# Later merge pieces, an earlier query norm, and an expert choice cut in pieces, in a two-block transformer kernel

## The chip, the cores and the metric

The kernel runs on one core of one Trainium2 chip. The time is the device time of one execution, in microseconds (us). The core has five engines with queues of their own: TensorE (PE, matmuls and transposes; its weight loads are listed as PEld), VectorE (DVE), ScalarE (ACT), GpSimd (POOL in the profile) and SyncE (SP, which only issues DMAs). Each works through its own queue in order and waits on the others through semaphores.

## What is computed

Two blocks over 1024 tokens of width 1024, in float32. The first has a mixer with two branches and a layer of 32 experts; the second has another mixer and a layer of 64 experts with a shared one. Cut to what matters here:

```python
# first block
xa = causal_conv(x_rnn, conv_w, conv_b)
ya = rg_lru(xa, ...) * gelu(g_rnn)
q = rms_norm(((rms_norm(q_c) @ w_uq)).reshape(B, S, 16, 96), q_norm_g)   # 16 heads
k = rms_norm(concat([k_nope, k_pe]), k_norm_g)
q, k = rope on the last 32 of 96
yb = chunk_causal_attention(q, k, v)
merged = gates[0] * ya + gates[1] * yb
h = h + merged @ w_out
h = h + hier_moe(rms_norm(h), ...)            # 32 experts in 4 groups, top 2
# second block
mix = concat([hgrn2(q, k, v, f) normed and gated, multiscale_pool(u) @ w_pool])
h = layer_norm(h * ALPHA + mix @ w_out)
scores = sigmoid(h @ w_router); sel = scores + bias
# the 4 best of 8 groups, then the 8 best experts in them, weights normed
h = layer_norm(h * ALPHA + moe_ffn(h))        # 64 experts, top 8, and a shared expert
```

## The kernel before

The stages follow one another, each with its own pools of tiles; a tile in a new pool lies where older ones lay and waits for their last readers. Each engine runs its instructions in the order of the program text, with semaphores between the engines. Products in which precision matters are made of three float32r matmuls (`mm3`): each operand is split in a high part (a rounding copy, mostly on ACT, L247) and a low part (the difference, mostly on DVE, L253).

**Queries and keys.** Eight chunks of weights, keys and queries in turn, are multiplied with the latents; each chunk gives 4 heads for 1024 tokens. The norm of a chunk's half (`post_q`) is a generator of a few steps: mean square, root, scaling and rope, and the store to `q_d` on SP. The steps are taken one at a time between later tiles. The function that holds all this is itself a generator: it yields once, attention sets up and does its first head, and then it goes on. In the kernel before the yield comes ahead of the last steps, and the last half's rope is on DVE; the others are on GpSimd.

**Attention.** It loads k, q and v of a pair of heads (`load`), reads the norm weights of q and k into `gk`, splits transposed pieces (`t_piece`), and computes for head n + 1 the maxima of the scores (`m_piece`, tile tm, reduces into nm on DVE) beside the scores of head n. A head has eight tile rows kt; for each, `s_mm` makes scores in PSUM (st, three buffers) and ACT takes the exps (L950). `row_piece` (L929) closes the maxima of a head, once in each head's period. After an odd head, the pair before is merged with the gates and the recurrent branch in six parts: 0 and 1 scale by 1/sum, 2 and 3 apply the gates (DVE, L994 and L996), 4 copies the result to mgh (ACT, two of 128x512, L999), 5 writes the remainder mgl (DVE, L1002). The table MERGE says for each part from which head on and at which kt; `rec` fetches the next head's 1/sum.

**First expert layer.** The route runs on DVE while the first expert's weights, loaded ahead, are split in six pieces (four of gate and up, two of down). START and ORDER say how many pieces stand ahead of each step of the route and in which order the rest goes (s a piece, o one-hot tables, w the second columns of the slot table, x transposes); LOD0 names the pieces whose low part is made on DVE, the others are on GpSimd.

**Second mixer and its projection.** `mixer2` has pools hc (v and others), hw (weights) and more; they lie where the staging tiles s0 to s2 of w_out come to lie again. `mixer_out2` loads w_out through these tiles in eight pieces (s, L2388, split to woh and wol), and goes over ten steps t: two half tiles of the product and the sum with the residual (L2461), `trans(t - 2)` behind the first and `router(t - 2)` behind the second, then `norm(t)`, whose root is on ACT (rsa_t, L291). `route2` chooses experts for four token tiles at a time; for tiles 0 to 3 it runs whole behind router(3).

Of the kernel before, what the change touches and what calls it, by code (L numbers as in the profile page):

```python
# [231 lines left out]
class Body:  # L232
# [429 lines left out]
    def qkv(self):  # L662
# [5 lines left out]
        with ExitStack() as cx:  # L668
# [111 lines left out]
            for i in range(8):  # L780
# [27 lines left out]
                else:  # L808
                    qn = ep.tile([128, 8, 4, 96], F32, name="qn", tag="kq", bufs=3)
                    dst = self.q_d[c].rearrange("(t p) c -> p t c", p=128)  # L810
                    for t in range(8):
# [11 lines left out]
                            step()  # L823
                        if t == 3:
                            posts.append(post_q(qn, sq, 0, dst, nc.gpsimd))
                    posts.append(post_q(qn, sq, 4, dst, nc.vector if i == 7 else nc.gpsimd))
            pc.close()
            yield
            while posts:
                step()  # L830

    MERGE = (2, 0), (3, 0), (3, 0), (3, 1), (3, 1), (3, 2)

    def attention(self, rb, rk, ml):

# [3 lines left out]
        with ExitStack() as cx:  # L839
# [37 lines left out]
            room(1)  # L877
            load(0)
            load(1)
            gk = k0.tile([96, 3], F32, name="gk")  # L880
            for i, nme in enumerate(("q_norm_g", "k_norm_g")):
                a = IN[nme]
                nc.scalar.dma_start(gk[:, i:i + 1], bass.AP(tensor=a.tensor, offset=a.offset, ap=[[1, 96], [1, 1]]))
            sc = 96 ** -0.5
            nc.vector.memset(gk[64:96, 0:2], 1.0)
            nc.vector.tensor_mul(gk[:, 2:3], gk[:, 0:1], gk[:, 1:2])
# [180 lines left out]
            def beside(h, kt):  # L1067

                n = h + 1
                fill = []  # L1070
                if kt == 0 and h % 2:
                    load(h // 2 + 2)
                if n < 16:
                    if kt < 2:
                        fill += [(t_piece, n, "kq"[kt], half) for half in range(2)]
                    fill += [(m_piece, n, i, a) for i, a in
                             {3: [(7, 0), (7, 512), (6, 0)], 4: [(6, 512), (5, 0), (5, 512)],
                              5: [(4, 0), (4, 512), (3, 0)], 6: [(2, 0), (1, 0), (0, 0)]}.get(kt, ())]
                    if kt == 5:
                        fill.append((v_piece, n))  # L1080
                    if kt == 7:
                        fill += [(lambda: None,), (row_piece, n)]
                if kt == (3 if h == 15 else 4) and h > 0:
                    fill.append((rec, h - 1))
                if h == 15 and kt == 6:
                    fill.append((merge, 7, 0, 0, 2, nc.vector))
                for part, (late, at) in enumerate(self.MERGE):
                    if h >= late and (h - late) % 2 == 0 and kt == at:
                        fill.append((merge, (h - late) // 2, part, 0, 2, nc.vector if part else nc.gpsimd))
                return fill  # L1090

            self.wo, self.W = {}, {}
# [161 lines left out]


    def moe_consts(self):
        nc, c = self.nc, self.const
        self.before = c.tile([128, 128], BF, name="before")
        nc.vector.tensor_scalar(self.before, self.jp, 0.0, None, op0=OP.is_gt)
# [692 lines left out]
    CAP1 = 96  # L1952
    RAW1, RAW2 = 13, 11
    DBUFS = 1, 1
    START, ORDER = (1, 1, 2, 0), "oswsSSx"
    YACT = 5
    LOD = (0, 2, 5), (0, 3, 5)
    LOD0 = (5,), (1, 3)

    def shared_place(self, j):  # L1960
        return self.sh.tile([128, 2048], F32, name=f"s{(j + 1) % 3}")
# [86 lines left out]
    def mixer2(self, u2):  # L2048

        nc, tc, IN = self.nc, self.tc, self.IN  # L2050
        win = IN["w_in_2"][0]
        with ExitStack() as cx:
            c1 = cx.enter_context(tc.tile_pool(reuse_waits="tile", name="hc", bufs=1))
            wp = cx.enter_context(tc.tile_pool(reuse_waits="tile", name="hw", bufs=2))
            sp = cx.enter_context(tc.tile_pool(reuse_waits="tile", name="hs", bufs=10))
            ep = cx.enter_context(tc.tile_pool(reuse_waits="tile", name="he", bufs=1))
            up = u2.enter_context(tc.tile_pool(reuse_waits="tile", name="u2", bufs=1, side="right"))
# [273 lines left out]
            self.mgh = mix.tile([128, 8, S], F32R, name="mxh")  # L2331
            self.mgl = mix.tile([128, 8, S], F32R, name="mxl")
            with tc.tile_pool(reuse_waits="tile", name="hq", bufs=2, space=PSUM) as pp, tc.tile_pool(reuse_waits="tile", name="hqt", bufs=4, space=PSUM) as pt:
                wpl = wp.tile([128, 4, 128], F32, name="w")
                nc.sync.dma_start(wpl, IN["w_pool_2"][0].rearrange("g c d -> c g d"))
                wplh = wp.tile([128, 4, 128], F32R, name="wh")
                wpll = wp.tile([128, 4, 128], F32R, name="wl")
                self.split(wpl, wplh, wpll)
                hg = c1.tile([128, 4], F32, name="hg")
                nc.vector.tensor_scalar(hg, self.v("hg_norm_g_2", 0, 4), 0.5, None, op0=OP.mult)  # L2340
# [25 lines left out]
    def mixer_out2(self, mo):  # L2366
# [5 lines left out]
        with ExitStack() as cx:  # L2372
# [58 lines left out]
            def router(t):  # L2431
                xT, xf = X.pop(("T", t)), X.pop(("f", t))
                pl = pt.tile([128, 512], F32, name="tp")
                for k in range(8):
                    nc.tensor.matmul(pl[:, 0:64], xT[:, k], rw[:, k], start=k == 0, stop=k == 7)
                nc.scalar.activation(lg[t // 4][:, t % 4], pl[:, 0:64], AF.Copy)
                ah = ep.tile([128, D], F32, name="ah", bufs=1)
                nc.scalar.activation(self.plain(ah), self.turned(xf), AF.Copy, scale=self.ALPHA)
                (nc.gpsimd if t > 4 else nc.sync).dma_start(self.acc_d[t * 128:t * 128 + 128], ah)
                if t == 3:  # L2440
                    for _ in self.route2(rtp, lg[0], bias, 0, 4):
                        pass
            self.route_late = lambda rp: self.route2(rp, lg[1], bias, 4, 8)
            self.pre2 = {}

# [2 lines left out]
            for t in range(10):  # L2448
# [4 lines left out]
                for half in range(2):  # L2453
                    if t < 8:
# [4 lines left out]
                                     [(self.mgh[:, k, ts_], self.mgl[:, k, ts_], h[:, k], lo[:, k]) for k in range(8)])  # L2459
                        hs = X[t][:, half * 512:half * 512 + 512]  # L2460
                        nc.vector.scalar_tensor_tensor(hs, hs, self.ALPHA, ps, op0=OP.mult, op1=OP.add)  # L2461
                    if t > 1:
                        (router if half else trans)(t - 2)
                if t < 8:
                    norm(t)
                    loadx(t + 2)


    def route2(self, rp, lg, bias, t0, t1):
# [286 lines left out]
```

## Time and profile before

| | us |
|---|---|
| three runs | 3194.46, 3202.43, 3207.52; median 3202.43 |
| the profiled execution | 3195.43 |
| its span in the trace | 3193.6 |

The stages, by the trace: recurrent branch to 475, latents to 570, queries and keys to 722, attention to about 1075, output projection and first route to 1229, 32 experts to 1586, second mixer to 1970, its projection to 2121, 64 experts to 3160, and the last norms.

In the rows, PEclk is the clock that TensorE was granted as a share of full speed; a matmul at half clock takes up to twice as long. "idle before <- X" names what ended the engine's idle time just before the instruction. Buffer numbers are left out of names.

### The profile page before, as it was taken

Reading aid. Unit: us, or ns where it says so; the run is one execution under the profiler, and the core shown is the slowest. Engines: PE = TensorE matmul, PEld = TensorE weight load, DVE = VectorE, ACT = ScalarE, POOL = GpSimd, SP = SyncE. Lnnn points to the kernel's source line nnn. Section 1 sums busy time; section 2 is a strip of 40 time slices with the busy share of each in tenths; the row PEclk is TensorE's granted clock in tenths of the full one; section 3 lists DMA queues with packets and bytes.
Section 4 is the critical chain, followed back from the end, with each engine's and each line's share of the span. In section 5 each row is a group of like instructions: output and inputs, shape, how many; then the busy total and the mean of one; then the engine's idle time right before and its main releaser. Section 6 shows DMA issues by size and latency. Waiting matters only on the chain. (4 is left out here: it accounts for less than half of the span.)

```text
span 3193.6 us, 41876 instructions
## 1 busy us (share of the span) xinstructions
PE 2953.0 (92%) x15865; PEld 2183.8 (68%) x15865; DVE 1814.7 (57%) x2909; ACT 1249.6 (39%) x1929; POOL 642.9 (20%) x495
## 2 busy tenths in 40 slices
PE   5999999998999996999889998978999999999995
PEld 4778778896666893655479787955666666666663
DVE  5545651666666656566446565445655555555556
ACT  3332332444445323444343324332344444444343
POOL 0000000121000103233212232112233232333320
PEclk9999999998999997999989999979999999999997
DMA  3212120244332267999720102337899999999994
GB/s 115 66 53 86 66 73 23 97 163 110 93 93 90 92 219 275 300 330 351 239 104 28 40 18 90 132 137 242 267 282 322 303 327 313 316 316 323 314 307 144
DMA packets 225885, 579.71 MB, mean 182 GB/s; under 512 B 22421, under 2 KB 104005, under 8 KB 225653
## 3 DMA queue, kind: packets, MB, share of 16 engines
q1 hardware_dynamic: 187952, 444.37, 39.6%
q0 software_dynamic: 37296, 132.55, 16.6%
q8 instruction: 127, 2.08, 0.3%
q14 instruction: 78, 0.64, 0.1%
q10 hardware_dynamic: 432, 0.06, 0.0%
HBM read 470.22 MB, written 106.64 MB: 181 GB/s over the span
## 5 line engine op out<-in xcount | busy, mean ns | idle before, releaser
L271 PE MATMUL mm<-uh,wh 128*128 128x512 f32 x640 | 252.6, 395 | 10.8 <-ACT t L505 8.8
L273 PE MATMUL mm<-uh,wl 128*128 128x512 f32 x640 | 251.8, 393 | 0.0
L272 PE MATMUL mm<-ul,wh 128*128 128x512 f32 x640 | 251.7, 393 | 0.0
L1475 PE MATMUL gups<-raw,x 128*128 128x512 f32 (+1 forms) x536 | 236.4, 592 | 0.0
L1622 ACT ACTIVATE th<-gups 128x128 f32<-128x128 f32 (+2 forms) x136 | 49.0, 361 | 418.9 <-PE gups L1475 251.0
L1691 POOL DMA_INDIRECT acc_d<-y,si x68 | 118.3, 1740 | 438.9 <-DMA acc_d<-y,si 145.9
L1623 DVE SCALAR_TENSOR_TENSOR hh<-th,gups 128x128 f32<-128x128 f32 (+2 forms) x136 | 53.1, 390 | 241.9 <-ACT th L1622 235.7
L253 DVE TENSOR_TENSOR gl<-raw,gh 128x1024 fp32r<-128x1024 f32 x142 | 168.1, 1221 | 28.4 <-ACT gh L247 28.3
L1688 DVE TENSOR_SCALAR y<-yps,wsl 128x512 f32<-128x512 f32 (+1 forms) x95 | 71.2, 750 | 196.7 <-ACT y L1686 193.8
L271 PE MATMUL gups<-gh,xh 128*128 128x512 f32 (+1 forms) x440 | 179.8, 409 | 0.9 <-ACT xh L1589 0.9
L1686 ACT ACTIVATE y<-yps,wsl 128x512 f32<-128x512 f32 (+1 forms) x100 | 68.7, 687 | 276.9 <-PE yps L1475 146.9
L273 PE MATMUL gups<-gh,xl 128*128 128x512 f32 (+1 forms) x440 | 176.4, 401 | 0.0
L272 PE MATMUL gups<-gl,xh 128*128 128x512 f32 (+1 forms) x440 | 176.1, 400 | 0.0
L1475 PEld LDWEIGHTS gups<-raw,x 128*128 128x128 f32 (+1 forms) x536 | 95.3, 183 | 116.4 <-issue 116.4
L1579 PEld LDWEIGHTS tp<-ident,xg 128*128 128x128 f32 (+2 forms) x1088 | 114.2, 144 | 74.6 <-issue 38.5
L958 PE MATMUL o<-raw,v 128*128 128x512 f32 (+3 forms) x384 | 163.4, 514 | 0.0
L271 PEld LDWEIGHTS mm<-uh,wh 128*128 128x128 f32 x640 | 121.7, 190 | 38.1 <-ACT t L505 10.6
L247 ACT ACTIVATE gh<-raw 128x1024 fp32r<-128x1024 f32 x142 | 142.9, 1054 | 10.5 <-PE gups L273 7.7
L1579 PE MATMUL tp<-ident,xg 128*128 128x128 f32 (+2 forms) x1088 | 128.5, 262 | 15.5 <-DMA xg<-xf_d,gi 7.1
L273 PEld LDWEIGHTS mm<-uh,wl 128*128 128x128 f32 x640 | 121.6, 190 | 25.7
L272 PEld LDWEIGHTS mm<-ul,wh 128*128 128x128 f32 x640 | 121.7, 190 | 25.3
L950 ACT ACTIVATE raw<-st 128x512 f32<-128x512 f32 (+1 forms) x192 | 92.8, 490 | 117.8 <-PE st L949 116.7
(685 smaller groups left out, 7669.0 us busy)
## 6 DMA issues: line engine op xcount, KB each, us to landing
raw<-in_w_down_dram SPq DMA_DIRECT2D x69, 1024.0 KB
raw<-in_w_gate_dram SPq DMA_DIRECT2D x136, 512.0 KB
raw<-in_w_up_dram SPq DMA_DIRECT2D x136, 512.0 KB
w<-in_w_in_dram SPq DMA_DIRECT2D x20, 1024.0 KB
s<-in_w_down_dram SPq DMA_DIRECT2D x17, 1024.0 KB
s<-in_w_gate_dram SPq DMA_DIRECT2D x34, 512.0 KB
s<-in_w_up_dram SPq DMA_DIRECT2D x34, 512.0 KB
b<-in_w_gate_dram SPq DMA_DIRECT2D x22, 512.0 KB
```

Source lines behind the costliest of these rows:

```text
L247: nc.scalar.activation(hi, src, AF.Copy)
L253: e.tensor_tensor(lo, src, hi.bitcast(F32), op=OP.subtract)
L271: nc.tensor.matmul(out, lh, rh, start=start and i == 0, stop=False, **kw)
L272: nc.tensor.matmul(out, lh, rl, start=False, stop=False, **kw)
L273: nc.tensor.matmul(out, ll, rh, start=False, stop=stop and i == n - 1, **kw)
L950: nc.scalar.activation(raw[:, a - kt * 128:b - kt * 128], st, AF.Exp)
L958: nc.tensor.matmul(O[h][a // 512][:, a % 512:a % 512 + b - a], v, p[:, a - kt * 128:b - kt * 128], start=kt == 0, stop=kt == (7 if a >= 51 ...
L1475: nc.tensor.matmul(out, x, w, start=start and i == 0, stop=stop and i == len(pairs) - 1, **kw)
L1579: nc.tensor.transpose(ps[:, k // 4, (k % 4) * R:(k % 4) * R + R], xg[:R, k * 128:k * 128 + 128], self.ident[:R, :R])
L1686: nc.scalar.activation(y[:R, 0:512], ps[0][:R], AF.Copy, scale=w)
L1688: nc.vector.tensor_scalar(y[:R, 512:1024], ps[1][:R], w, None, op0=OP.mult)
L1691: nc.gpsimd.indirect_dma_start(out=acc_d, out_offset=bass.IndirectOffsetOnAxis(ap=si, axis=0), in_=y[:R], in_offset=None, compute_op=OP.add)
```

## The change

Five things change.

1. MERGE: part 4 moves from kt 1 to kt 3 and part 5 from kt 2 to kt 4; in one kt the merge's parts now stand ahead of `rec`.
2. The last steps of the norms of q stand ahead of the yield, the last half's rope is on GpSimd like the others, and gk's loads move to the setup.
3. START, ORDER and LOD0: the first expert's pieces 0 and 1 stand at the route's start with low parts on GpSimd, pieces 2 to 5 have theirs on DVE. The pieces of expert 1 (S) are gone from ORDER; expert 1 is split whole in both kernels.
4. In mixer2 the pool hw is opened ahead of hc, and the pooling weights go through a slot of another pool instead of hw.
5. In mixer_out2 the expert choice of tiles 0 to 3 is taken in pieces: three steps after norm(5), three after norm(6), the rest in step 7; trans(6) stands ahead of norm(7).

```diff
--- before.py
+++ after.py
@@ -823,13 +823,13 @@
                             step()
                         if t == 3:
                             posts.append(post_q(qn, sq, 0, dst, nc.gpsimd))
-                    posts.append(post_q(qn, sq, 4, dst, nc.vector if i == 7 else nc.gpsimd))
+                    posts.append(post_q(qn, sq, 4, dst, nc.gpsimd))
             pc.close()
-            yield
             while posts:
                 step()
-
-    MERGE = (2, 0), (3, 0), (3, 0), (3, 1), (3, 1), (3, 2)
+            yield
+
+    MERGE = (2, 0), (3, 0), (3, 0), (3, 1), (3, 3), (3, 4)
 
     def attention(self, rb, rk, ml):
 
@@ -877,10 +877,7 @@
             room(1)
             load(0)
             load(1)
-            gk = k0.tile([96, 3], F32, name="gk")
-            for i, nme in enumerate(("q_norm_g", "k_norm_g")):
-                a = IN[nme]
-                nc.scalar.dma_start(gk[:, i:i + 1], bass.AP(tensor=a.tensor, offset=a.offset, ap=[[1, 96], [1, 1]]))
+            gk = self.gk
             sc = 96 ** -0.5
             nc.vector.memset(gk[64:96, 0:2], 1.0)
             nc.vector.tensor_mul(gk[:, 2:3], gk[:, 0:1], gk[:, 1:2])
@@ -1080,13 +1077,13 @@
                         fill.append((v_piece, n))
                     if kt == 7:
                         fill += [(lambda: None,), (row_piece, n)]
+                for part, (late, at) in enumerate(self.MERGE):
+                    if h >= late and (h - late) % 2 == 0 and kt == at:
+                        fill.append((merge, (h - late) // 2, part, 0, 2, nc.vector if part else nc.gpsimd))
                 if kt == (3 if h == 15 else 4) and h > 0:
                     fill.append((rec, h - 1))
                 if h == 15 and kt == 6:
                     fill.append((merge, 7, 0, 0, 2, nc.vector))
-                for part, (late, at) in enumerate(self.MERGE):
-                    if h >= late and (h - late) % 2 == 0 and kt == at:
-                        fill.append((merge, (h - late) // 2, part, 0, 2, nc.vector if part else nc.gpsimd))
                 return fill
 
             self.wo, self.W = {}, {}
@@ -1254,6 +1251,10 @@
 
 
     def moe_consts(self):
+        self.gk = self.const.tile([96, 3], F32, name="gk")
+        for i, nme in enumerate(("q_norm_g", "k_norm_g")):
+            a = self.IN[nme]
+            self.nc.scalar.dma_start(self.gk[:, i:i + 1], bass.AP(tensor=a.tensor, offset=a.offset, ap=[[1, 96], [1, 1]]))
         nc, c = self.nc, self.const
         self.before = c.tile([128, 128], BF, name="before")
         nc.vector.tensor_scalar(self.before, self.jp, 0.0, None, op0=OP.is_gt)
@@ -1952,10 +1953,10 @@
     CAP1 = 96
     RAW1, RAW2 = 13, 11
     DBUFS = 1, 1
-    START, ORDER = (1, 1, 2, 0), "oswsSSx"
+    START, ORDER = (2, 0, 0, 0), "osswxss"
     YACT = 5
     LOD = (0, 2, 5), (0, 3, 5)
-    LOD0 = (5,), (1, 3)
+    LOD0 = (2, 3, 4, 5), (1, 3)
 
     def shared_place(self, j):
         return self.sh.tile([128, 2048], F32, name=f"s{(j + 1) % 3}")
@@ -2050,8 +2051,9 @@
         nc, tc, IN = self.nc, self.tc, self.IN
         win = IN["w_in_2"][0]
         with ExitStack() as cx:
+
+            wp = cx.enter_context(tc.tile_pool(reuse_waits="tile", name="hw", bufs=2))
             c1 = cx.enter_context(tc.tile_pool(reuse_waits="tile", name="hc", bufs=1))
-            wp = cx.enter_context(tc.tile_pool(reuse_waits="tile", name="hw", bufs=2))
             sp = cx.enter_context(tc.tile_pool(reuse_waits="tile", name="hs", bufs=10))
             ep = cx.enter_context(tc.tile_pool(reuse_waits="tile", name="he", bufs=1))
             up = u2.enter_context(tc.tile_pool(reuse_waits="tile", name="u2", bufs=1, side="right"))
@@ -2331,10 +2333,9 @@
             self.mgh = mix.tile([128, 8, S], F32R, name="mxh")
             self.mgl = mix.tile([128, 8, S], F32R, name="mxl")
             with tc.tile_pool(reuse_waits="tile", name="hq", bufs=2, space=PSUM) as pp, tc.tile_pool(reuse_waits="tile", name="hqt", bufs=4, space=PSUM) as pt:
-                wpl = wp.tile([128, 4, 128], F32, name="w")
+                wpl = slot()[:, :512].rearrange("p (g d) -> p g d", g=4)
                 nc.sync.dma_start(wpl, IN["w_pool_2"][0].rearrange("g c d -> c g d"))
-                wplh = wp.tile([128, 4, 128], F32R, name="wh")
-                wpll = wp.tile([128, 4, 128], F32R, name="wl")
+                wplh, wpll = [z[:, a] for z in [slot(F32R).rearrange("p (a g d) -> p a g d", a=2, g=4)] for a in range(2)]
                 self.split(wpl, wplh, wpll)
                 hg = c1.tile([128, 4], F32, name="hg")
                 nc.vector.tensor_scalar(hg, self.v("hg_norm_g_2", 0, 4), 0.5, None, op0=OP.mult)
@@ -2437,9 +2438,12 @@
                 ah = ep.tile([128, D], F32, name="ah", bufs=1)
                 nc.scalar.activation(self.plain(ah), self.turned(xf), AF.Copy, scale=self.ALPHA)
                 (nc.gpsimd if t > 4 else nc.sync).dma_start(self.acc_d[t * 128:t * 128 + 128], ah)
-                if t == 3:
-                    for _ in self.route2(rtp, lg[0], bias, 0, 4):
-                        pass
+            first = self.route2(rtp, lg[0], bias, 0, 4)
+
+            def advance(n):
+                for _ in range(n):
+                    next(first, None)
+
             self.route_late = lambda rp: self.route2(rp, lg[1], bias, 4, 8)
             self.pre2 = {}
 
@@ -2459,11 +2463,16 @@
                                      [(self.mgh[:, k, ts_], self.mgl[:, k, ts_], h[:, k], lo[:, k]) for k in range(8)])
                         hs = X[t][:, half * 512:half * 512 + 512]
                         nc.vector.scalar_tensor_tensor(hs, hs, self.ALPHA, ps, op0=OP.mult, op1=OP.add)
-                    if t > 1:
+                    if t > 1 and (half or t != 8):
                         (router if half else trans)(t - 2)
+                    if t == 7 and not half:
+                        advance(1)
+                if t == 7:
+                    trans(6)
                 if t < 8:
                     norm(t)
                     loadx(t + 2)
+                    advance({5: 3, 6: 3}.get(t, 0))
 
 
     def route2(self, rp, lg, bias, t0, t1):
```

On ACT in head 3 of attention, before and then after the change: raw are the exps, mgh the merge's copies, y the copy of a finished head.

```order
L262 ACTIVATE kq_4615<-tm,gk 96x512 x2
L950 ACTIVATE raw<-st 128x512
L999 ACTIVATE mgh_4740<-rec 128x512
L999 ACTIVATE mgh_4742<-rec 128x512
L950 ACTIVATE raw<-st 128x256
L950 ACTIVATE raw<-st 128x512
L971 ACTIVATE y<-o_5195 128x512
L950 ACTIVATE raw<-st 128x128
L950 ACTIVATE raw<-st 128x512 x2
```

```order
L262 ACTIVATE kq_4639<-tm,gk 96x512 x2
L947 ACTIVATE raw<-st 128x512
L947 ACTIVATE raw<-st 128x256
L947 ACTIVATE raw<-st 128x512
L968 ACTIVATE y<-o_5195 128x512
L947 ACTIVATE raw<-st 128x128
L947 ACTIVATE raw<-st 128x512
L996 ACTIVATE mgh_4740<-rec 128x512
L996 ACTIVATE mgh_4742<-rec 128x512
L947 ACTIVATE raw<-st 128x512
L947 ACTIVATE raw<-st 128x384
```

The two copies moved from behind one exp of tile row 1 to the end of row 3, with four exps and the copy y now ahead of them.

On SP where attention starts, before and then after: q_d and k_d are in memory, b are the tiles of the first two pairs.

```order
L806 DMA v_d_3164<-vv 128x8x256
L749 DMA k_d_3160<-kn 128x4x384
L862 DMA b_4594<-k_d_3157 128x8x192
L862 DMA b_4593<-q_d_3153 128x8x192
L865 DMA b_4594<-v_d_3161 128x4x128
L865 DMA b_4593<-v_d_3161 128x4x128
L862 DMA b_4592<-k_d_3157 128x8x192
L862 DMA b_4591<-q_d_3153 128x8x192
```

```order
L806 DMA v_d_3167<-vv 128x8x256
L749 DMA k_d_3163<-kn 128x4x384
L767 DMA q_d_3159<-qn 128x4x384 x2
L862 DMA b_4621<-k_d_3160 128x8x192
L862 DMA b_4620<-q_d_3156 128x8x192
L865 DMA b_4621<-v_d_3164 128x4x128
L865 DMA b_4620<-v_d_3164 128x4x128
L862 DMA b_4619<-k_d_3160 128x8x192
```

The two stores of the last q chunk, which stood behind all loads, now stand ahead of them.

On DVE in the second output projection, before and then after: bst, bmv, bvar, brs and bnb belong to a norm, xf is its result, W and ex are the end of the expert choice, sc and sel its start.

```order
L2516 TENSOR_TENSOR W_15816<-W_15816,ex 128x256
L2517 CAST ex<-W_15816 128x256
L2407 BN_STATS bst<-xr 128x6 x2
L2408 BN_AGGR bmv<-bst 128x2
L2410 TENSOR_SCALAR bvar<-bmv 128x1
L292 RECIPROCAL brs<-rsa_t 128x1
```

```order
L296 TENSOR_TENSOR brs<-brs,rsa_t 128x1
L2413 SCALAR_TENSOR_TENSOR bnb<-bmv,brs 128x1
L2416 TENSOR_TENSOR xf<-xf,g 128x1024
L2485 TENSOR_SCALAR sc<-sc 128x256
L2486 TENSOR_TENSOR sel<-sc,rbias 128x256
L2492 MAX m_15785<-sel 128x8 x32
```

Norm 5 stood behind the last row of the choice; now the first row of the choice stands behind norm 5.

## Rows read from the trace of the kernel before

**Rows 1.** the page, busy time of each engine, its share of the span, and instructions.

```profile
PE 2953.0 (92%) x15865; PEld 2183.8 (68%) x15865; DVE 1814.7 (57%) x2909; ACT 1249.6 (39%) x1929; POOL 642.9 (20%) x495
```

**Rows 2.** windows: stretch, length, busy us (instructions) by engine, granted clock, DMA share, GB/s.

```profile
2300.00:3150.00 850.00, 847.51 (x4698) 531.05 (x4697) 480.77 (x674) 359.91 (x541) 253.75 (x173) 1.00 0.97 303
```

**Rows 3.** waits of PE in attention: line, awaited, us in all, times, longest.

```profile
PE st L947 <- ACT raw L950: 16.2, 7, 2.6
PE tm L901 <- DVE kq L260: 4.5, 2, 3.7
```

**Rows 4.** windows in attention: a plain head, one with a merge, eleven heads.

```profile
788.84:807.67 18.83, 18.83 (x97) 13.96 (x96) 11.77 (x27) 10.28 (x21) 2.35 (x1) 1.00 0.05 16
891.98:913.64 21.66, 19.09 (x97) 14.01 (x96) 16.36 (x32) 11.07 (x23) 0.00 (x0) 1.00 0.55 159
807.67:1042.53 234.86, 219.43 (x1057) 159.26 (x1056) 157.02 (x327) 118.18 (x243) 11.75 (x5) 0.95 0.32 94
```

**Rows 5.** timeline, ACT and DVE, of head 3 of attention: start, length, idle before.

```profile
816.70 1.15 ACT L999 ACTIVATE mgh<-rec 128x512 fp32r<-128x512 f32 x2 [2.29 <-DVE rec L996]
815.46 1.21 DVE L996 SCALAR_TENSOR_TENSOR rec<-m,rec 128x1024 f32<-128x1024 f32 x1
817.37 1.29 DVE L1002 SCALAR_TENSOR_TENSOR mgl<-rec,mgh 128x512 fp32r<-128x512 f32 x2 [0.70 <-ACT mgh L999]
```

**Rows 6.** timeline of SP, PE, GpSimd and DVE where attention starts; last a window.

```profile
722.25 0.36 SPq L862 DMA_DIRECT2D b<-q_d  x1
728.40 1.09 PE L901 MATMUL tm<-ident,b 128*96 128x128 f32 x4 [5.30 <-DMA b<-q_d]
720.12 1.29 POOL L763 TENSOR_TENSOR qg<-qn,gr 128x512 f32<-128x512 f32 x1 [16.43 <-DVE qn L761]
725.29 0.72 POOL L725 TENSOR_TENSOR qn<-rt,rt 128x256 f32<-128x256 f32 x1
742.93 1.75 DVE L755 TENSOR_REDUCE ms<-sqq 128x16 f32<-128x1536 f32 x1
746.30 1.76 DVE L761 TENSOR_TENSOR qn<-qn,rs 128x1536 f32<-128x1536 f32 x1
751.00:762.00 11.00, 9.23 (x24) 6.54 (x25) 5.40 (x9) 5.25 (x11) 1.07 (x2) 0.53 0.71 180
```

**Rows 7.** timeline of DVE and GpSimd in the first route.

```profile
1203.36 0.17 DVE L1305 TENSOR_TENSOR y<-y 128x16 f32<-128x16 f32 x1
1203.57 2.24 DVE L1308 TENSOR_SCALAR y<-y 128x16 f32<-128x16 f32 x1
1203.44 2.34 POOL L253 TENSOR_TENSOR gl<-b,gh 128x1024 fp32r<-128x1024 f32 x1 [2.65 <-ACT gh L247]
1222.15 3.04 DVE L1379 TENSOR_TENSOR y<-y,cols 128x128 f32<-128x128 f32 x1
1227.31 1.22 DVE L253 TENSOR_TENSOR dl<-b,dh 128x1024 fp32r<-128x1024 f32 x1
```

**Rows 8.** loads of w_out on SP, wait of PE, window, second mixer's end.

```profile
1968.51 13.89 SPq L2388 DMA_DIRECT2D s<-in_w_out_dram  x8
PE mm L271 <- ACT woh L247: 3.3, 1, 3.3
1972.00:1992.00 20.00, 14.15 (x66) 12.98 (x67) 10.90 (x10) 9.71 (x9) 1.73 (x4) 0.66 1.00 329
```

**Rows 9.** timeline of DVE and ACT, wait of PE, window, second output projection.

```profile
2067.68 0.29 DVE L2476 TENSOR_SCALAR sc<-sc 128x256 f32<-128x256 f32 x1 [5.15 <-ACT sc L2475]
2080.27 1.28 DVE L2407 BATCH_NORM_STATS2 bst<-xr 128x6 f32<-128x512 f32 x2
2082.01 0.20 ACT L291 ACTIVATE rsa_t<-bvar 128x1 f32<-128x1 f32 x1 [13.06 <-DVE bvar L2410]
PE tp L2435 <- ACT xT L2429: 16.2, 3, 10.3
2076.00:2093.00 17.00, 6.83 (x33) 6.83 (x34) 12.02 (x34) 5.64 (x7) 2.87 (x1) 0.60 0.09 30
```

## The prediction

> **What bounds the kernel now.** I read the page's busy line first: TensorE (PE) is busy for 92% of the span and no other engine for over 57% [rows 1]. The end of the span is therefore set by PE's work and by the places where PE stands still or runs at its lower clock. Then the table by stage. In the long stretch of the second expert layer PE has work for 847.51 of 850 us at full clock [rows 2]: everything behind the route of that layer is PE's own pace, so a microsecond that PE gains ahead of it should arrive at the end whole. The change touches no matmul, so I looked for gaps of PE in the five places that it touches, with the list of waits of PE for each stretch, and then for the granted clock beside them: where PE has stood idle the rows show half speed (1.2 instead of 2.4 GHz) for some microseconds, and these cost more than the gap itself.
>
> **Part 1, the merge's parts in attention.** In this stretch the dearest wait of PE is for the exps on ACT, 16.2 us in 7 gaps [rows 3]. One gap followed back: on ACT the copy mgh (L999) stands idle for 2.29 us until DVE's L996, which ends at 816.67, and the exps of the next tiles queue behind it; PE has three score buffers, fills them and stops [rows 5]. The period of a head, from one row_piece to the next, is 18.83 us without a merge; where the gap alone shows and the clock stays up it is 21.66, and mostly it is more, with half clock in part of it. Six such heads and five plain ones stand between 807.67 and 1042.53, 234.86 us at a mean clock of 0.95, so the six take 234.86 - 5 * 18.83 = 140.7 together, 23.45 each [rows 4]. The change puts the copies at the end of tile row 3, three rows of exps after L996, and mgl (1.29 us, [rows 5]) on DVE into row 4. Nothing waits for mgh but mgl, and nothing for mgl but the output projection and the next pair's gate loads, which are used two heads later. If the gap goes, its clock fall goes too: six heads at 19.1 (PE's own 19.09 in the head of full clock, [rows 4]) are 114.6, so 26.1 us are gained. Gaps alone would be 16.2 less the new waits, if any. DVE is the cover: it works 16.36 us in such a head [rows 4], which in 19.1 leaves 2.7; it already ran four of the merge's pieces in rows 0 to 2 without one PE wait for DVE, and loses one of them there to row 4. I take **-26**, from -27.7 to 0.
>
> **Part 2, the start of attention.** What is removed: the last q chunk's norm, which on DVE runs from 742.93 (L755) to 748.06 (L761 ends, so 5.1 us) and then has its rope there, in the middle of head 0's splits; PE waits 3.7 us for one of these [rows 3], and from 751 to 762 PE works 9.23 us at a clock of 0.53 [rows 6], which is some 4 us more than at full clock. What is added: two stores to q_d now stand on SP ahead of the first loads of k and q, and SP works in order. Before, the q load was issued at 722.25 and PE had it at 728.40, 6.15 us later [rows 6]. Now the second store waits for the last chunk: last projection matmul about 722.2 (the q load, whose tile waits for that memory, is issued at once), ACT's copies 1.2 (two of 128x512 took 1.15, [rows 5]), the chain on DVE 5.1, the rope on GpSimd 5.9 (720.12 to 726.01 for the same seven operations of the chunk before, [rows 6]): 734.4. Behind it the q load, issued at about 735.4, lands at 741.6 by its own 6.15 us, or at 743 to 744 if store, k and q load (0.79 MB each by their shapes) share the 303 GB/s of [rows 2] from 735 on. That is 13 to 16 us later than now, for PE nearly all idle. Given back: the 3.7 us, the 4 us of clock, and half a microsecond for the norm weights, which are then long in place. I take +15 - 8 = **+7**, from +3 (early landing and all given back) to +14 (late landing, the clock not back).
>
> **Part 3, the first route.** GpSimd splits the first expert's weights (2.34 us each) while DVE runs the route. The rows show DVE held for as long: L1305 takes 0.17 us and its like L1308 2.24, until GpSimd's split that began at 1203.44 is over; L1379 takes 3.04 under the split of dl [rows 7]. There are four such holds in the route (L1329 and L1494 have the others), some 8 us together; the splits that cause them go from GpSimd. Two splits move onto DVE ahead of the slot table's last columns, 1.22 each [rows 7]: -8 + 2.4 = -5.7. Against it stands that q1's split now follows q0's at once, and would lie on DVE's L1293 and what follows (about 2 us): -3.7. The trace has no split there, so both stay. I take **-4**, from -8 to +2.
> The Trainium skill has a rule on such holds, in "SBUF — State Buffer", section "SBUF: two separate sides": VectorE and GpSimd share a port pair as an exclusive lock, and the loser blocks for the whole instruction; of VectorE's instructions, those with two SBUF inputs are among them. L1308's row agrees in length. By the rule q1's split holds L1293 too, and this part gives -3.7; without it -5.7. The sum goes by neither alone.
>
> **Part 4, the second mixer's pools.** The eight loads of w_out are issued only at 1968.51, when the last transposes have read v, and ACT and PE wait for them in turn, PE 3.3 us in one gap, with the clock at 0.66 from 1972 to 1992 [rows 8]. With the pools exchanged the staging tiles lie over the projection's weight buffers, free since the last projection, some 10 us earlier. The gap (3.3) and some 3 us of the lost clock go; w_pool's split, now in a reused slot, starts up to 1.4 us later ahead of PE's first pool matmul. I take **-5**, from -8 to 0.
>
> **Part 5, the second output projection.** The whole expert choice of the first half runs on DVE from 2067.68 to 2080.27 in one piece ahead of norm 5; ACT waits 13.06 us at norm 5's root with the copies xT behind it, and PE waits 16.2 us in three gaps, 10.3 the longest, with a clock of 0.60 from 2076 to 2093 [rows 9]. In the new order norm 5 comes first, then 5 us of the choice, norm 6, 5 us, one half's sum, 2 us, norm 7. DVE does as much as before, so what is gained is the time in which it now stands idle (ACT's and PE's turns in norms 5 to 7): counting DVE's queue through from 2062.5, norm 7 starts some 9 to 10 us earlier than now. I take **-9**, from -5 to -12;
>
> **The sum:** -26 + 7 - 4 - 5 - 9 = -37 us. The profiled execution took 3195.4 us, so 3158.4 by its own time; the median of the runs, 3202.4, lies 7 us above it, and I carry the difference to it: **3165.4**.
>
> **The rivals.**
> - *The stall only moves* (12%). ACT's copies at row 3 still find the exps behind them, or DVE's mgl at row 4 holds the reduces that free PE's buffers, and each odd head keeps one gap of the present price. Part 1 is 0, the rest -11: 3191. For it: DVE has 2.7 us to spare in such a head. Against it: L996 is done two rows before, and exps have their buffers full by then.
> - *Two stalls for one* (5%, the slower side). In rows 3 and 4 of the six odd heads PE stops for mgh and again for the reduces behind mgl. One stall now costs 23.45 - 18.83 = 4.6 us a head with its clock [rows 4], so a second one adds 27.7: 3202.4 + 27.7 - 11 = 3219. The point from which it decides is 11 / 6 = 1.8 us a head beyond the present stall; below that the other parts outweigh it. For it: the same 2.7 us that DVE has to spare, and two queues instead of one. Against it: DVE's lag in rows 0 to 2 makes PE wait nowhere now.
> - *The gaps close, the clock stays down* (13%). The half-clock stretches have other small gaps beside them; parts 1, 4 and 5 give their gaps alone, part 2 gets no clock back: -16 + 11 - 4 - 4 - 6 = -19: 3183.
> - *The weights aren't there earlier* (6%). In the last stage DMA is at 0.97 [rows 2]; if the experts' weights set the pace after all, the 14 us of parts 4 and 5 turn into waits of PE: 3180. Against it: PE has no such wait there now.
> - *The norm ahead doesn't get ahead* (4%). If GpSimd's rope is held as DVE's operations were in part 3, the stores leave at 750 and attention starts 16 us later yet: 3181.
>
> **How the numbers follow.** The forecast has 60%, with its own range 3154 to 3178. Faster by over 0.5% (below 3186.4; half a percent is about what a measurement of this kernel tells from no change) holds nearly all of it and most of the third, fourth and fifth: 0.77. Within 0.5%: the first rival and the rest of these: 0.18. Slower: 0.05. The range runs from 3153 (all parts but the second at their better ends, -27.7 + 7 - 8 - 8 - 12 = -49) to 3191 (the first rival).
>
> **What would show it.** Right: odd heads of 19 to 19.5 us at clock 1.00, no PE wait for L950; PE idle from 723 to 742 or so and no wait of 3.7 us later; L1308 and L1379 back at 0.2 to 0.4 us and the first expert's first matmul some 23 us earlier; w_out's loads some 10 us ahead of the last transposes; ACT's wait of 13 us gone. Wrong: PE waiting for nm's reduces or for mgh's exps in rows 3 to 5; the first loads landing past 750; PE waits for weights in the second expert layer.

## The result and the profile after

| | before | after |
|---|---|---|
| median of the runs, us | 3201.61 (4) | 3168.97 (4) |
| lowest, highest | 3194.46, 3207.52 | 3163.48, 3170.53 |
| the profiled execution | 3195.43 | 3168.84 |
| its span | 3193.6 | 3166.9 |

The ratio of the times is 0.9896, with a 95% interval from 0.9872 to 0.9920: faster by 1.0%, 26 to 41 us. The forecast was 3165.4. Two executions took far longer than all others of their kernel, 6742.55 us of the kernel before and 3498.84 us of the one with part 3 alone, and no ratio contains them.

In all kernels of this document PE runs the same 15865 instructions in the same order, so the start of each can be subtracted from its start in the kernel before. This gives the time gained up to any place. For the changed kernel:

| place | start before | shift |
|---|---|---|
| last projection matmul of q | 721.9 | +1.1 |
| head 3 of attention | 813.6 | +12.4 |
| head 14 | 1042.8 | -12.3 |
| first route | 1194.8 | -12.9 |
| first expert | 1233.8 | -14.4 |
| end of the first expert layer | 1553.6 | -11.9 |
| last matmuls of the second mixer | 1954.9 | -13.6 |
| in the second projection | 2021.6 | -21.1 |
| start of the second expert layer | 2161.0 | -28.1 |
| near its end | 3139.7 | -26.9 |

Such a shift compares one execution with one. The profiled execution of the kernel before lies 6 us under its median, and kernels that leave a stretch as it was show shifts of their own there, from -1.2 to +2.9 us. A gain over one stretch is therefore good to some 3 us.

The waits of PE in the changed kernel, by line and awaited instruction (us in all, times, longest), first from 700 to 1075:

```profile
PE tm L898 <- DMA b<-k_d: 20.2, 1, 20.2
PE tm L898 <- DMA b<-q_d: 5.2, 1, 5.2
PE tm L926 <- DVE mz L922: 3.3, 7, 1.6
```

The same view from 1945 to 2100:

```profile
PE tp L2429 <- DVE xf L2417: 12.6, 1, 12.6
...
PE mm L271 <- ACT woh L247: 2.1, 1, 2.1
```

Of the 16.2 us in [rows 3] for the exps nothing is left. In their place stand waits of 20.2 and 5.2 us where attention starts, and one of 12.6 us at the end of the second projection. The windows of the changed kernel, with the columns of [rows 2]: the same eleven heads as in the last line of [rows 4], and the first head with a merge among them:

```profile
820.08:1030.22 210.14, 208.51 (x1058) 153.44 (x1056) 155.95 (x327) 118.31 (x243) 11.82 (x5) 1.00 0.35 105
820.08:839.37 19.29, 19.02 (x97) 13.90 (x95) 16.19 (x32) 11.15 (x23) 0.00 (x0) 1.00 0.62 177
```

234.86 us have become 210.14, and the mean clock 1.00 instead of 0.95.

### The profile page after: what moved, and what is told of

It reads as the page before. It is cut to its first block, busy times and chain, and to the rows that moved or that the text cites. A ratio compares the mean times of both kernels' runs of the same rounds, so it can differ in the third digit from the quotient of the medians.

```text
span 3166.9 us, 41876 instructions
## 1 busy us (share of the span) xinstructions
PE 2932.1 (93%) x15865; PEld 2168.2 (68%) x15865; DVE 1811.8 (57%) x2905; ACT 1251.0 (40%) x1929; POOL 640.0 (20%) x499
## 5 line engine op out<-in xcount | busy, mean ns | idle before, releaser
L955 PE MATMUL o<-raw,v 128*128 128x512 f32 (+3 forms) x384 | 155.2, 492 | 0.0
```

The costliest lines, as they stand in the source:

```text
L955: nc.tensor.matmul(O[h][a // 512][:, a % 512:a % 512 + b - a], v, p[:, a - kt * 128:b - kt * 128], start=kt == 0, stop=kt == (7 if a >= 51 ...
```

## The experiments

The parts alone, each put into the kernel before, as they stand in the diff; then changes to the changed kernel. All times are medians; the ratio is to the kernel before in the same comparison. The interval of the changed kernel's ratio is 8 us to either side, and those of its variants are hardly narrower. Where such a variant differs from the changed kernel by less than some 11 us, the times alone do not show it, and the trace is given beside them.

**Part 1 alone.** 

> The kernel before with part 1 alone (the merge's last two pieces later). Theory: the stall for the exps and the half clock behind it go, and nothing after attention takes them back: six heads at 19.1 instead of 23.45 us, so 25 to 26 us off the end, about 3176 us. Rival A, the stall only moves: 3202. Rival B, gaps close but the clock still falls: 16 us off, 3186. In the trace: no wait of PE for L950, clock 1.00 from 808 to 1042 by the theory, 0.95 by rival B.

3172.62 us, ratio 0.9925 (0.9907 to 0.9943). PE is 0.5 us ahead at head 3 and 25.5 at head 14: 25.0 us in eleven heads, and 24 to 27 ahead from there to the end. PE has no wait for L950, and the eleven heads run at full clock, as this window of the kernel with part 1 alone shows:

```profile
807.10:1018.00 210.90, 209.28 (x1067) 154.25 (x1066) 156.24 (x328) 118.88 (x244) 11.85 (x6) 1.00 0.35 105
```

Six of the seven gaps of [rows 3], of 2.57 us each, lie in these heads, 15.4 us together; in their place stand 1.6 us of short waits. So 14 of the 25 us are gaps, and the other 11 are the half clock that followed them in five of the six heads (in the one of 21.66 us in [rows 4] it did not). Rivals A and B fall. The new order of the merge's parts and `rec` is in this run, too; it was not tried apart.

**Part 2 alone.** 

> The kernel before with part 2 alone (last q norm ahead, its stores ahead of the first loads). Theory: the first loads leave some 14 us later, land some 15 to 20 us later because store and both loads share the transfer, and half of it comes back where the norm no longer cuts head 0: 12 us later at head 1 and at the end, 3214 us. Rival, my sum before the result: 7 us, 3209. Rival B, the time is made up later in attention or by the weights of the first expert layer being there already: 3202.

3211.00 us, ratio 1.0042 (1.0025 to 1.0059): slower, as the theory says, by 13 us (8 to 19). PE is 12.7 us later at head 3 than at the last projection matmul, and nothing later takes that back. So one part of the change costs what half of another brings. How it costs is in the changed kernel's timeline of SP (start, length, DMAs in a row):

```profile
727.12 8.84 SPq L767 DMA_DIRECT2D q_d<-qn  x2
736.02 0.50 SPq L862 DMA_DIRECT2D b<-k_d  x1
736.62 1.16 SPq L862 DMA_DIRECT2D b<-q_d  x1
```

The first transposes of k and of q in its timeline of PE:

```profile
743.45 1.91 PE L898 MATMUL tm<-ident,b 128*96 128x128 f32 x8 [20.16 <-DMA b<-k_d]
750.52 1.94 PE L898 MATMUL tm<-ident,b 128*96 128x128 f32 x8 [5.17 <-DMA b<-q_d]
```

SP stands 8.84 us at the stores, the second of which waits for the end of the rope, as the changed kernel's timeline of GpSimd shows:

```profile
734.86 0.72 POOL L725 TENSOR_TENSOR qn<-rt,rt 128x256 f32<-128x256 f32 x1
```

The first loads go out behind them at 736.02 and 736.62, where the q load of [rows 6] went at 722.25; the k load takes 7.4 us to PE and the q load 13.9.

**The stores behind the loads.** In the changed kernel:

```diff
+            late = []
...
-                nc.sync.dma_start(dst[:, t0:t1], q.rearrange("p t h d -> p t (h d)"))
+                store = lambda: nc.sync.dma_start(dst[:, t0:t1], q.rearrange("p t h d -> p t (h d)"))
+                if last:
+                    late.append(store)
+                else:
+                    store()
...
             while posts:
                 step()
             yield
+            for store in late:
+                store()
...
-                nc.gpsimd.dma_start(kq[96:NR], self.reach_d)
+                (nc.gpsimd if i else nc.scalar).dma_start(kq[96:NR] if i else kq[96:NR].bitcast(F32), self.reach_d if i else self.reach_d.bitcast(F32))
...
-                nc.gpsimd.memset(z, LOW)
+                nc.vector.memset(z, LOW)
```

`last` is set for both halves of the last q chunk. The last two edits take a small load and a fill of head 0 out of GpSimd's queue, where they stand behind the rope.

> The changed kernel, with the last chunk's norm still ahead of attention's setup but its two stores to q_d behind the first loads on SP; for this the small fills in front of head 0 go to DVE and the rows of reach for head 0 are fetched from ACT's queue, so that they don't wait behind the rope on GpSimd. Theory: the loads behind the stores alone make the start late; PE starts head 0 at 728 to 730 as before and keeps what part 2 gives back: 20 us less than the changed kernel, 3149 us. Rival, the norm's chain on DVE and GpSimd itself holds head 0's splits: 3160 to 3169.

3150.03 us, ratio 0.9835 (0.9812 to 0.9859), 19 us below the changed kernel: the theory's figure, less one. PE gets its first q at 727.59, and what part 2 gives back stays, so that head 3 is 9.3 us earlier than in the kernel before. The first transposes of q in its timeline of PE:

```profile
727.59 1.06 PE L906 MATMUL tm<-ident,b 128*96 128x128 f32 x4 [4.22 <-DMA b<-q_d]
```

The window of the same kernel over the end of head 0:

```profile
750.00:762.00 12.00, 12.00 (x55) 7.97 (x55) 8.56 (x22) 4.09 (x9) 0.00 (x0) 1.00 0.06 8
```

This is the stretch that ran at 0.53 in [rows 6], now at 1.00. The norm's chain on DVE and GpSimd holds nothing that PE waits for. What the stores bring without the other two edits was not tried; in the changed kernel PE's two waits are for the loads of k and q.

**Without part 2.** 

> The changed kernel without part 2 (parts 1, 3, 4 and 5). Theory, parts add: 12 us less than the changed kernel, 3157 us. Rival, part 2's loss is hidden later (weights, gathers): as the changed kernel, 3169.

3156.36 us, ratio 0.9864 (0.9841 to 0.9886): 12.6 us below the changed kernel by the medians, 12.3 by the traces near the end. The parts add: alone, by their traces, they come to 12.7 - 25.0 - 1.2 - 5.8 - 8.6 = -27.9, together to -26.9. Part 2 as it stands is a loss.

**Part 3 alone.** 

> The kernel before with part 3 alone (first expert's low parts off GpSimd in the route). Theory: the slot table's last columns come 3 us earlier, but the first gather's issue on GpSimd takes over 5 us instead of 3.3 and PE waits 3 us for it, and the next gathers wait as long as before: 0 to 2 us off, 3200 to 3202. Rival, my sum: 4 us off, 3198.

3196.77 us, ratio 0.9985 (0.9972 to 0.9998). The interval, 1 to 9 us, holds both. The trace tells more: PE gains 1.5 us between the first route (+3.2) and the first expert (+1.6), and 1.2 of it are left at the end of the layer. The four kernels with one other part alone lose 0.8 to 1.1 and 1.6 to 2.7 us there against the same trace, so part 3 is worth some 2 us, no more than such shifts differ by among themselves. The changed kernel's timeline of DVE in the route:

```profile
1188.21 0.17 DVE L1293 TENSOR_REDUCE y<-lg 128x4 f32<-128x16 f32 x1
1188.41 2.11 DVE L1294 TENSOR_TENSOR y<-lg,y 128x16 f32<-128x16 f32 x1
...
1191.92 0.17 DVE L1309 TENSOR_SCALAR y<-y 128x16 f32<-128x16 f32 x1
...
1202.20 0.95 DVE L1495 TENSOR_TENSOR y<-slot_r,pos 128x768 bf16<-128x768 f16 x1
1203.07 2.35 DVE L253 TENSOR_TENSOR gl<-b,gh 128x1024 fp32r<-128x1024 f32 x2
...
1207.43 0.33 DVE L1380 TENSOR_TENSOR y<-y,cols 128x128 f32<-128x128 f32 x1
```

And of GpSimd:

```profile
1185.84 4.65 POOL L253 TENSOR_TENSOR gl<-b,gh 128x1024 fp32r<-128x1024 f32 x2 [1.86 <-ACT gh L247]
1201.10 5.58 POOL L1570 DMA_INDIRECT xg<-xf_d,gi  x1 [10.62 <-DMA raw<-in_w_gate_dram]
1206.99 0.92 POOL L1570 DMA_INDIRECT xg<-xf_d,gi  x1 [0.30 <-issue]
```

The holds of [rows 7] are gone: L1309 and L1380 (L1308 and L1379 there) take 0.17 and 0.33 us. But L1294 now takes 2.11, until GpSimd's two splits of 4.65 are over, while the reduce just ahead of it (L1293) takes 0.17 under the same splits, and the issue of the first gather takes 5.58 us on GpSimd while DVE splits gl beside it. PE then waits 3.0 us for the gathered rows:

```profile
1212.26 1.54 PE L1580 MATMUL tp<-ident,xg 96*128 96x96 f32 x8 [2.99 <-DMA xg<-xf_d,gi]
```

**The table's columns ahead of the splits.** In the changed kernel:

```diff
-    START, ORDER = (2, 0, 0, 0), "osswxss"
+    START, ORDER = (2, 0, 0, 0), "owssxss"
```

> The changed kernel with the slot table's last columns ahead of the two splits that moved to DVE. Theory: the first gather's issue on GpSimd is held by these two splits; without them beside it it takes some 3.3 us as before instead of 5.6, and PE's wait of 3.0 us for the gather falls below 1. Rival: the issue's length has to do with DVE's one-hot tables, which stay beside it: 5.6 us as in the changed kernel. At the end of the first expert layer nothing changes by either.

One run, 3159.45 us, too few to tell such a difference by time. The issue of the gather is 3.31 us long, as this kernel's timeline of GpSimd shows:

```profile
1201.11 3.31 POOL L1570 DMA_INDIRECT xg<-xf_d,gi  x1 [10.62 <-DMA raw<-in_w_gate_dram]
```

PE's wait for it, in its timeline of PE, is 0.99:

```profile
1208.00 1.54 PE L1580 MATMUL tp<-ident,xg 96*128 96x96 f32 x8 [0.99 <-DMA xg<-xf_d,gi]
```

So the splits stretched it by 2.3 us. The other traces agree: the issue is 5.58 us long in all six kernels with the splits beside it, and 3.31 or 3.32 in all seven without. In the changed kernel and in this one the issue ends 1.26 us behind a row of long DVE operations: 1205.42 to 1206.68 behind the splits in the changed kernel, 1203.16 to 1204.42 behind the one-hot tables (L1495) here, and an issue with neither beside it takes 0.92. The tables seem to hold it likewise, so the rival is half right; that was not tried by itself, nor why DVE's operations hold it. The last sentence of the expectation was wrong: PE is 5.3 us further ahead at the first expert than at the route and still 5.1 at the end of the layer, where the changed kernel has lost what it gained.

**Part 4 alone.** 

> The kernel before with part 4 alone (pools exchanged in the second mixer). Theory: w_out's loads leave before the last transposes, PE's gaps in front of the second projection and the clock fall behind them go: 9 us off, 3193 us. Rival, my sum before the result: 5 us, 3197. Rival B, the weights of the second expert layer set the pace of the last stage: 3202 and waits of PE there.

3192.44 us, ratio 0.9984 (0.9969 to 0.9999). By the trace 5.8 us are gained from the second mixer's last matmuls to the second projection (7.5 in the changed kernel, 5.8 without part 2), and 4.8 are left near the end. The interval, 0.3 to 10 us, holds both figures. My sum's 5 was nearer than the 9 of the expectation, which came from one trace. The loads of [rows 8] in the changed kernel's timeline of SP:

```profile
1942.35 22.05 SPq L2389 DMA_DIRECT2D s<-in_w_out_dram  x8
```

They leave 18 us ahead of the second projection's first matmul at 1960.37; before, it was 4.6 (1968.51 to 1973.08). The window over this place, with the clock at 0.91 where [rows 8] have 0.66:

```profile
1955.00:1975.00 20.00, 16.24 (x116) 15.21 (x115) 16.04 (x16) 13.47 (x15) 1.61 (x3) 0.91 0.51 171
```

**Part 5 alone.** 

> The kernel before with part 5 alone (expert choice in pieces). Theory: PE gains some 17 us through norms 5 and 6 and loses 11 to 12 again in one gap ahead of the last transposes, which wait for norm 7 behind the choice's last pieces: 6 us off, 3196 us. Rival, my sum: 9 us off, 3193. In the trace: two of DVE's small operations in the choice held for 2 to 3 us while GpSimd adds the norm's bias.

3191.66 us, ratio 0.9980 (0.9964 to 0.9995). By the trace 8.6 us are gained up to the second expert layer (7.0 in the changed kernel, 5.7 without part 2), so both figures lie in what the traces show. The changed kernel's timeline of DVE:

```profile
2050.78 3.23 DVE L2486 TENSOR_TENSOR sel<-sc,rbias 128x256 f32<-128x256 f32 x1
...
2067.85 2.53 DVE L2505 TENSOR_SCALAR gm<-gm 128x32 f32<-128x32 f32 x1
...
2078.14 1.28 DVE L2408 BATCH_NORM_STATS2 bst<-xr 128x6 f32<-128x512 f32 x2
```

Beside these, in its timeline of GpSimd, the bias additions of norms 5 and 6:

```profile
2050.68 3.05 POOL L2417 TENSOR_TENSOR xf<-xf,b 128x1024 f32<-128x1024 f32 x1 [10.95 <-DVE xf L2416]
2067.43 2.91 POOL L2417 TENSOR_TENSOR xf<-xf,b 128x1024 f32<-128x1024 f32 x1 [13.70 <-issue]
```

And its window over the wait for norm 7:

```profile
2075.00:2095.00 20.00, 7.44 (x34) 6.60 (x33) 9.58 (x20) 7.33 (x8) 1.06 (x2) 0.50 0.14 57
```

Two operations of 0.43 and 0.18 us as the trace of before has them (L2477 and L2496 there) take 3.23 and 2.53. Norm 7's statistics start at 2078.14, behind the choice's pieces, and PE waits 12.6 us for its result and then runs at half clock.

**The additions on DVE.** In the changed kernel:

```diff
-                (nc.vector if t == 7 else nc.gpsimd).tensor_tensor(...)
+                (nc.vector if t in (5, 6, 7) else nc.gpsimd).tensor_tensor(...)
```

> The changed kernel with the bias addition of norms 5 and 6 on DVE instead of GpSimd (2.0 us each there, 3.0 on GpSimd). Theory: two operations of the choice (the bias of the scores, 3.23 us, and the mask, 2.53) are held by these additions; they fall to 0.4 and 0.2, and with 4 us of additions and 5.2 us of holds gone norm 7 starts about 1 us earlier. Rival, the two are long for another reason (the wait for the scores from ACT): they stay long, and norm 7 starts 4 us later.

This kernel's timeline of DVE, the statistics of norms 5 and 7 and the two operations:

```profile
2039.23 1.28 DVE L2407 BATCH_NORM_STATS2 bst<-xr 128x6 f32<-128x512 f32 x2
...
2051.05 0.43 DVE L2485 TENSOR_TENSOR sel<-sc,rbias 128x256 f32<-128x256 f32 x1
...
2067.48 0.29 DVE L2504 TENSOR_SCALAR gm<-gm 128x32 f32<-128x32 f32 x1
...
2075.53 1.28 DVE L2407 BATCH_NORM_STATS2 bst<-xr 128x6 f32<-128x512 f32 x2
```

One run, 3161.97 us. The two are back at 0.43 and 0.29 us: GpSimd's additions held them. The median of the changed kernel lies 7 us above, but one run cannot show that as a gain. From norm 5's statistics to norm 7's it is 36.3 us, 36.9 in the changed kernel (2041.21 to 2078.14): 0.6 us, about as expected, since the additions cost DVE nearly what the holds did.

**The choice's rest behind norm 7.** In the changed kernel:

```diff
-                    if t == 7 and not half:
-                        advance(1)
...
-                    advance({5: 3, 6: 3}.get(t, 0))
+                    advance({5: 3, 7: 4}.get(t, 0))
```

> The changed kernel with the last four pieces of the choice behind norm 7 instead of behind norm 6 and in step 7. Theory: norm 7, on which PE waits 12.6 us in the changed kernel, starts about 9 us earlier, and the pieces run while PE does the last transposes and the router: that gap falls to 4 to 6 us, and the end comes 6 to 8 us earlier than the changed kernel's, 3161 to 3163. Rival: the pieces then hold the second half's choice and PE waits for it at the start of the second expert layer instead: 3169.

3160.27 us, ratio 0.9878 (0.9853 to 0.9903), 8.7 us below the changed kernel by the medians, 6 by the ratios; neither is clear of the noise, but the trace is: PE gains 13.6 us in the second projection instead of 7.0, and the gap is down to 5.9, in this kernel's waits of PE:

```profile
PE tp L2428 <- DVE xf L2416: 5.9, 1, 5.9
```

PE waits nowhere longer at the start of the second expert layer, where its longest wait is 3.8 us here and 4.1 in the changed kernel, both for the same gather.

**All three mends.** The changed kernel with the stores behind the loads, the columns ahead of the splits and the choice's rest behind norm 7. 

> The changed kernel with all three mends: stores behind the first loads (19 us off in its own run), the slot table's columns ahead of the splits (4 to 5 us at the first expert's start by its trace), and the choice's last pieces behind norm 7. Theory, they add: 26 to 31 us less than the changed kernel, 3138 to 3143 us. Rival, the later ones are absorbed by gathers and weights in the expert layers: as with the stores alone, 3150.

3137.52 us (3134.50 to 3144.12), ratio 0.9802 (0.9783 to 0.9822). This is 31.5 us below the changed kernel and 63 below the one before. The mends add: at the start of the second expert layer the three gain 16.0, 5.3 and 10.5 us by their traces, 31.7 in all, and together 31.5.

## Why the prediction was right, and where not

The forecast, its sign and its size held: 3165.4 against 3168.97. The sum was -37; the medians fell by 32.6. The two traces alone give less, -26.9 near the end: the profiled execution of the kernel before was a quick one, 6 us under its median, and the changed kernel's lies at its median. So it was right to lay the sum on the median, with the 7 us that I carried over, and not on the profiled execution, though one trace could not show that.

To take the quick execution out, the last column of the table uses all traces. For each part it takes the stretch in which the part acts, between two places of the first table (head 3 to 14; projection to head 3; route to the end of its layer; second mixer to second projection; from there to the second expert layer). It is the mean shift over it in the kernels that have the part as it stands in the change, less the mean in those that don't have it, the one before included.

| part | forecast | trace of the changed kernel | alone, by its trace | all traces |
|---|---|---|---|---|
| 1, merge | -26 | -24.7 | -25.0 | -26.0 |
| 2, start of attention | +7 | +11.4 | +12.7 | +12.1 |
| 3, first route, to its layer's end | -4 | +1.0 (-1.5 at the first expert) | -1.2 (-1.5) | -2.0 |
| 4, pools | -5 | -7.5 | -5.8 | -7.4 |
| 5, choice | -9 | -7.0 | -8.6 | -8.3 |

The last column adds up to -31.6, and the medians say -32.6. So the parts went about as they were forecast, but for part 2, which cost 5 us more. Part 3 brought 2 less, and part 4, which brought 2 more, hides some of this in the total; that the forecast came within 4 us is in part luck.

*Part 1* went as worked out: heads with a merge take 19.29 us where I put 19.1, with a wait of 0.27 for mz in each. DVE as cover was enough.

*Part 2* is the term that was mis-sized. The stores and the q load left nearly when I had put it, the load at 736.62 for 735.4. But PE had it at 750.52, 22 us later than before, where I had it land at 741.6 to 744, 13 to 16 us later; "the first loads landing past 750", one of my own signs of being wrong, came true for it. The k load, which I had in the sum by its bytes alone, moved furthest. The timeline of SP in the kernel before has it ahead of the q load:

```profile
711.02 0.56 SPq L862 DMA_DIRECT2D b<-k_d  x1
```

So it had landed under the last projection, where now PE stands still from 723.29 with no transpose of head 0 done. And the q load took 13.9 us behind the k load and the store, where I let all three share 303 GB/s. Two windows of the changed kernel, between the first loads' issue and PE's first q:

```profile
736.00:744.00 8.00, 0.56 (x3) 0.57 (x4) 0.00 (x0) 0.00 (x0) 2.38 (x5) 0.50 1.04 242
744.00:751.00 7.00, 1.83 (x10) 1.35 (x9) 1.37 (x2) 1.19 (x2) 0.00 (x0) 0.50 1.10 202
```

The DMA engines were busy throughout and moved 242 and 202 GB/s; a rate read from the expert layers did not hold for these loads. The two windows make 3.35 MB, where store, k and q load are 2.36; so other loads shared the time, which I had left out. SP issued those of v and of the next pair from 737.83 on. What part 2 gives back was 8.7 us where I had 8: waits of 20.2 + 5.2 - 5.3 for the loads, less the 11.4 that are left.

*Part 3*: the four holds went as costed (-8 + 2.4 is -5.6 and not the -5.7 of the prediction, which changes nothing), and q1's split lay on L1294 (L1293 before) for 2.11 us, the 2 us of my own bound. What I had no term for is the first gather's issue on GpSimd: the two splits that I put on DVE at 1.22 us each also stretch it by 2.3 us, and PE waits there. The Trainium skill, "SBUF — State Buffer", section "SBUF: two separate sides", warns that VectorE can keep GpSimd from writing the descriptors of its DMAs, and names operations that hold both of VectorE's port pairs, copies of float32 above all. Here the operations beside the issue are subtractions of two tiles, which it does not name there, and the issue takes 5.58 us with them and 3.31 without: by the measurement, an indirect gather's issue is held by these, too. I weighed the rule's first half, on DVE, and not this one.

*Part 4* and *part 5* lie within their ranges. In part 4 the wait of 3.3 us for woh did not go whole, 2.1 are left at the first matmul; but another, which I had not named, went, in the waits of PE in the kernel before:

```profile
PE mm L271 <- DVE mxl L263: 3.3, 1, 3.3
```

In part 5 the same kind of hold cost 2.8 and 2.35 us on DVE ahead of norm 7, which I had not counted. The timeline of DVE in the kernel before has norm 7's statistics here:

```profile
2104.10 1.28 DVE L2407 BATCH_NORM_STATS2 bst<-xr 128x6 f32<-128x512 f32 x2
```

They now start at 2078.14, 26.0 us earlier; by 21.1 us of these PE was ahead in the second projection already. So norm 7 came 4.9 us earlier and not 9 to 10, and the two holds are the difference. The wait of 12.6 us for norm 7 had no row in the prediction.

Of the rivals none came true: the stall did not move, no second one appeared, the clock came back (1.00), the gains of parts 4 and 5 reached the end with no wait for weights, and the stores left by 736 and not at 750. Of the signs of being right one failed: the first expert started 14.4 us earlier and not 23, since part 2 cost more and part 3 gained less.

## What to carry to other kernels

A gap of PE in a loop can cost more than its length: here the end of six gaps, 15.4 us, brought 25, because the clock had fallen behind five of them. Before work is done earlier, look at what its last instruction does to an in-order queue: two stores that nobody waited for cost 20 us, as they stood ahead of loads. Between GpSimd and VectorE look at what runs beside, in both directions, gather issues included. And a trace is one execution: before two traces are subtracted, look at where each lies among the runs of its kernel.

## What the runs showed of the hardware

Some small DVE operations beside a GpSimd operation on two SBUF tiles lasted until that one was over: 0.2 to 0.4 us became 2.1 to 3.2. A reduce of 128x16 under the same splits kept its 0.17 us. The issue of an indirect gather on GpSimd took 3.31 us, and 5.58 with two DVE subtractions of 128x1024 beside it. Gaps of 2.57 us on PE were followed by half clock in five of six heads. The medians of the kernel before in the four comparisons, made on several chips, lay between 3199.67 and 3201.61, while its single runs, but for the one of 6742.55, spread over 23 us.
